# A two-layer encoder on one core: memory's keys and values ahead of the first projection, and row sums of the second layer taken from transposed quarters

## The chip, the core and the metric

The kernel runs on one core of a Trainium2 chip. The metric is the device time of one execution in microseconds (us). TensorE (PE in the profile; PEld are its weight loads) multiplies, VectorE (DVE) and ScalarE (ACT) work on whole tiles, GpSimd (POOL) does small arithmetic and issues the transfers that add while they move, and SyncE (SP) issues most loads and stores.

## What is computed

The input is 512 tokens by 1024 features, 256 memory tokens, and two layers of weights. Cut to what matters here:

```python
for i in range(2):
    h = rmsnorm(x, norm_g[i])
    mem_h = rmsnorm(mem, mem_norm_g[i])
    proj = einsum('bsd,de->bse', h, w_in)          # layer 0: 11264 columns, layer 1: 3584
    o_mix = mixer(...)                             # layer 0: dilated windows; layer 1: grouped queries with axial rotary
    kv = einsum('bnd,de->bne', mem_h, w_mem_kv[i]) # keys (normalized per head) and values of memory
    o_mem = attention(q_mem, k, v)
    y = concat([o_mix, o_mem]) * silu(gate)
    x = x + einsum('bse,ed->bsd', y, w_out[i])
```

Everything is float32. A product keeps that accuracy by splitting each operand into a high part (a rounded copy) and a low part (what the copy lost), and by summing three products: high by high, high by low, low by high.

## The kernel before

**Products.** `mm3` (lines 162 to 165) issues those three matmuls for one tile. A weight piece (128 x 1024, tile `wl`) is loaded, ACT makes its high part `wh` (`Weights.hi`, line 285), DVE its low part `wo` (`Weights.lo`, line 295). There are four buffers for `wh` and `wo`, so a cast waits until the matmuls of the piece four before it are done. Matmuls are issued in groups of twelve (128 x 512) or twenty-four (128 x 256); after each group `W.advance` issues the next pieces' low and high parts, sums and loads, and the driver's `tick` issues what is due of the evacuations, which are written as generators: `yield n` means "go on n groups later". All of it is one order written out by hand for each engine; each engine keeps to it.

**Seven products for eight.** The large projections (`s_chunk`) halve both operands in both directions and take seven products of quarters: of the activations the quarters 12, 11, 22 and the sums S1 to S4, of the weights the quarters 21, 11, 22 and the sums T1 to T4. Two pieces belong to each product when a chunk has 512 columns to a half (kinds W2 and W2s), one when it has 256. T2, T3 and T4 are made by transfers of POOL that add (lines 257, 264 and 269), T1 in layer 0 by DVE (line 251). In the very first chunk, number 0, DVE also makes T2 (line 259).

**Activations.** The blocks of x are normalized (`norm_1`: squares on ACT and three small operations on POOL; `norm_2`: two scalings of 128 x 512 on DVE, line 465). `turn4` transposes four 128 x 128 tiles on PE into one PSUM bank, ACT writes the high part (line 157), DVE the low part (line 160). `put_h` does that for one quarter of one pair of blocks. For S1 to S4 the sums are taken first, on the rows (`sum_h`, `sums_h`: DVE, lines 506 and 514 to 516), and each is then transposed as well: seven quarters by two blocks are 14 calls of `turn4`, 56 transposes, in either layer.

**The start.** x is loaded first, the first chunk is layer 0's projection of values (`ev_v0`, kind W2), and PE does `row_bank` (the gain row spread over 128 partitions by two matmuls of one row), transposes and then weights. Memory is loaded and normalized beside it (`mem_norm(0)`); its keys and values (`mem_kv`, two chunks of kind T2: two pieces for each of two units, two blocks) follow.

**Between the layers.** `out_rest` ends layer 0's output projection block by block, `ev_o` stores a block to `x1d`, normalizes it and puts its quarters, while PE works on memory's keys and values of layer 1 (two T2b chunks), and then on the seven products of memory's queries (24 matmuls of 128 x 256 to each). A small table for the rotary (`setup_b`, four DVE products) is made in the same place.

## Time and profile before

| | |
|---|---|
| median of 3 executions | 973.45 us (973.19 to 974.49) |
| the profiled execution, its own time | 971.6 us |
| span of it, first to last instruction | 969.8 us |
| PE busy | 949.5 us, 98% of the span |
| PEld, DVE, ACT, POOL busy | 835.8, 793.1, 675.4, 332.7 us |
| packets of SP's and ACT's queue, of POOL's | 43.5% and 32.5% of the 16 DMA engines' span |
| mean granted TensorE clock | 1.000 |

Matmuls overlap in the records: one of 128 x 512 is listed with 0.39 us while the next begins 0.23 us after it. So PE's pace is read from the starts of neighbouring rows, and idle time from what a view of the waits lists.

### The profile page before, as it was taken

The page shows a single profiled execution, that of the slowest core. Times are in us where ns is not written, and L with a number is a line of the kernel's source. Part 1 is how long each engine was busy: PE and PEld are TensorE (multiplying, and loading weights), DVE is VectorE, ACT ScalarE, POOL GpSimd, SP SyncE. Part 2 cuts the span into 40 slices and gives each one's busy share as a digit, 9 for nine tenths or more (in the row PEclk, how much of TensorE's full clock was granted, in tenths as well). Part 3 has the DMA queues.
Part 4 walks back from the last instruction along what each step waited for, and adds up shares of the span by engine and source line. Part 5 has one row for each costly group of instructions (what it writes and reads, how often), then busy time and mean ns, then how long its engine had stood idle before and what let it go on. Part 6 is the DMA issues. An engine that isn't in the chain of part 4 may idle for free. (4 is left out here: it accounts for less than half of the span.)

```text
span 969.8 us, 16665 instructions
## 1 busy us (share of the span) xinstructions
PE 949.5 (98%) x5728; PEld 835.8 (86%) x5728; DVE 793.1 (82%) x1413; ACT 675.4 (70%) x1687; POOL 332.7 (34%) x480
## 2 busy tenths in 40 slices
PE   8899999999999999999999999999999999999998
PEld 5689988888888888888899996787999999998776
DVE  6997776888888888888898999769888997779863
ACT  6555689686868686868685667545778887878760
POOL 1122423556454545454736011323233231011011
PEclk9999999999999999999999999999999999999999
DMA  8979846968787868685959889959986696786644
GB/s 331 326 267 336 220 102 170 293 131 259 150 256 154 256 153 261 154 260 131 279 134 233 259 203 272 299 191 351 240 178 148 178 241 166 218 213 163 183 140 130
DMA packets 88982, 209.27 MB, mean 216 GB/s; under 512 B 25281, under 2 KB 36033, under 8 KB 88898
## 3 DMA queue, kind: packets, MB, share of 16 engines
q1 hardware_dynamic: 70034, 146.28, 43.5%
q0 software_dynamic: 17568, 59.78, 32.5%
q10 hardware_dynamic: 1296, 2.16, 0.6%
q8 instruction: 45, 0.74, 0.3%
q14 instruction: 39, 0.32, 0.1%
HBM read 157.79 MB, written 12.65 MB: 176 GB/s over the span
## 5 line engine op out<-in xcount | busy, mean ns | idle before, releaser
L295 DVE TENSOR_TENSOR wo<-wl,wh 128x1024 fp32r<-128x1024 f32 x255 | 314.6, 1237 | 12.3 <-ACT wh L285 11.5
L285 ACT CAST wh<-wl 128x1024 fp32r<-128x1024 f32 x255 | 269.7, 1059 | 75.7 <-PE pj L165 39.8
L163 PE MATMUL pj<-wh,hS 128*128 128x512 f32 (+1 forms) x448 | 164.3, 367 | 0.0
L164 PE MATMUL pj<-wo,hS 128*128 128x512 f32 (+1 forms) x448 | 158.1, 353 | 2.6 <-DVE wo L295 2.6
L165 PE MATMUL pj<-wh,hS 128*128 128x512 f32 (+1 forms) x448 | 158.2, 353 | 0.0
L163 PE MATMUL pj<-wh,h 128*128 128x512 f32 (+1 forms) x336 | 123.4, 367 | 0.0
L164 PE MATMUL pj<-wo,h 128*128 128x512 f32 (+1 forms) x336 | 118.8, 354 | 2.3 <-DVE wo L295 2.3
L165 PE MATMUL pj<-wh,h 128*128 128x512 f32 (+1 forms) x336 | 118.9, 354 | 0.0
L420 POOL TENSOR_TENSOR rstd<-mse,half 128x4 f32<-128x4 f32 (+2 forms) x98 | 100.1, 1021 | 8.2
L164 PEld LDWEIGHTS pj<-wo,hS 128*128 128x128 f32 x448 | 85.0, 190 | 13.4 <-DVE wo L295 3.5
L165 PEld LDWEIGHTS pj<-wh,hS 128*128 128x128 f32 x448 | 84.7, 189 | 12.4 <-DVE hS L160 0.3
L163 PEld LDWEIGHTS pj<-wh,hS 128*128 128x128 f32 x448 | 84.8, 189 | 9.7
L419 POOL TENSOR_SCALAR mse<-hss 128x4 f32<-128x4 f32 (+1 forms) x86 | 44.3, 515 | 129.9 <-ACT junk L529 126.1
L360 ACT COPY sn<-pj 128x512 f32<-128x512 f32 x132 | 73.6, 591 | 14.3 <-PE pj L165 10.7
L529 ACT ACTIVATE junk<-sn 128x128 f32<-128x128 f32 x264 | 79.0, 308 | 0.2 <-DVE sn L371 0.2
L987 POOL TENSOR_TENSOR ta<-sn,tabs 128x128 f32<-128x128 f32 (+1 forms) x64 | 37.2, 584 | 119.7 <-DVE sn L534 91.6
L164 PEld LDWEIGHTS pj<-wo,h 128*128 128x128 f32 x336 | 64.0, 190 | 10.0 <-DVE wo L295 2.8
L165 PEld LDWEIGHTS pj<-wh,h 128*128 128x128 f32 x336 | 63.7, 190 | 9.3 <-DVE h L160 0.2
L163 PEld LDWEIGHTS pj<-wh,h 128*128 128x128 f32 x336 | 63.9, 190 | 7.3 <-ACT h L157 0.2
L377 DVE TENSOR_TENSOR sn<-pj,sn 128x512 f32<-128x512 f32 x99 | 67.5, 683 | 3.0 <-PE pj L165 2.6
L269 POOL DMA_DIRECT2D wl<-wl x33 | 29.3, 886 | 112.4 <-DVE wo L295 70.7
L163 PE MATMUL pj<-hS,wh 128*128 128x256 f32 x192 | 55.9, 291 | 0.0
(229 smaller groups left out, 2457.1 us busy)
## 6 DMA issues: line engine op xcount, KB each, us to landing
wl<-in_wall_dram SPq DMA_DIRECT2D x222, 512.0 KB, 6.9
wl<-wl POOLq DMA_DIRECT2D x64, 512.0 KB, 5.8
wl<-in_wall_dram POOLq DMA_DIRECT2D x42, 512.0 KB, 8.5
acc<-sn POOLq DMA_DIRECT2D x16, 256.0 KB, 5.0
od<-o SPq DMA_DIRECT2D x12, 256.0 KB, 5.2
og<-od SPq DMA_DIRECT2D x12, 256.0 KB, 6.8
odb<-o SPq DMA_DIRECT2D x12, 256.0 KB, 2.7
og<-odb SPq DMA_DIRECT2D x12, 256.0 KB, 3.9
```

The costliest lines, as they stand in the source:

```text
L163: T.matmul(o, lh, rh, start=start, stop=False, skip_group_check=True)
L164: T.matmul(o, lh, rl, start=False, stop=False, skip_group_check=True)
L165: T.matmul(o, ll, rh, start=False, stop=stop, skip_group_check=True)
L269: G.dma_start(self.tile[key], self.tile[c, "T2", x], accum_op=ALU.add)
L285: A.copy(wh, self.tile[self.items[i]])
L295: V.tensor_tensor(wo, self.tile[key], wh.bitcast(F32), ALU.subtract)
L360: A.copy(t, b)
L377: V.tensor_tensor(t, b, t, ALU.subtract if q == "12" else ALU.add)
L419: G.tensor_scalar(e, ss, EPS, None, ALU.add)
L420: G.tensor_tensor(r, e, half[:, 0:n], ALU.pow)
L529: A.activation(jk, p[:, j * 128:(j + 1) * 128], AF.Square, scale=QS, accum_out=ss[:, j:j + 1])
L987: G.tensor_tensor(ta[:, 0:n], xn[:, 0:n, 0:32], ropeA[:, 0, b, s0:s0 + n], ALU.mult)
```

## The change

It has these parts:

1. Memory's keys and values of layer 0 become PE's first work. Their rows and weights are loaded first (`SEQ` keeps the weights' places in memory, and changes the order of use), memory's gain row is spread first, x's gain row after it and copied to SBUF, memory is normalized at once, and x's blocks are normalized, transposed and summed in `prep` during memory's two chunks. The masks and rotary tables of layer 0 are loaded later, in `setup`.
2. `ev_v0`'s chunk follows. Its T2 sums are now made by POOL's transfer as in all other chunks; DVE's T1 stays.
3. In layer 1 only 12, 11, 22 and 21 are transposed: 8 calls of `turn4`. `first_t` keeps 12 and 11 as whole float32 tiles beside their high and low parts; `diffs_t` forms S1 = 21 - 22 and S3 = 11 - 21 from the transposed banks; `rest_t` makes S2 and S4 on whole tiles of 128 x 1024 and splits S2, S4, S3 and 22 in one piece of that size each.
4. In a chunk of memory or of the rest of an output projection, an evacuation is handed in before `W.advance` and its first step is issued before the next group's `W.advance` (`drv.release` for `drv.spawn`). The low part of memory's values is issued at the end of the same step as its high part, not a group later.
5. `EO` (gaps between the steps of `ev_o`), `SET_B` (when the rotary table of layer 1 starts), `PD`, `KEEP["T2"]` take other values.

```diff
-EO = 1, 2, 2, 2, 1
+EO = 2, 2, 1, 1, 1
+SEQ = [1, 2, 0] + list(range(3, len(PLAN)))
-KEEP = {"T2": 6, "T2b": 4, "O1": 4, "W1": 9, "W2": 10, "W2s": 9, "W1b": 7, "W2b": 9}
+KEEP = {"T2": 8, "T2b": 4, "O1": 4, "W1": 9, "W2": 10, "W2s": 9, "W1b": 7, "W2b": 9}
...
-                    if c:
-                        G.dma_start(self.tile[key], self.tile[c, "T1", x], accum_op=ALU.add)
-                    else:
-                        V.tensor_tensor(self.tile[key], self.tile[key], self.tile[c, "T1", x], ALU.add)
+                    G.dma_start(self.tile[key], self.tile[c, "T1", x], accum_op=ALU.add)
...
+                if pre:
+                    pre(u, b)
                 group(w, u, b, ps[b])
                 drv.free()
+                if u == units - 1:
+                    drv.release(evac(b, ps[b]), 2)
                 W.advance()
-                if u == units - 1:
-                    drv.spawn(evac(b, ps[b]), 2)
                 drv.tick()
...
+    def first_t(H, top, c):
+        ps = [(k, turn4(top[j], *slot(H, k, c))) for k, j in (("12", 1), ("11", 0))]
+        for k, p in ps:
+            A.copy(whole(k, c), p)
+
+    def diffs_t(H, low, c):
+        f22 = whole("22", c)
+        A.copy(f22, turn4(low[1], None, None))
+        p = turn4(low[0], None, None)
+        yield 1
+        s1, s3 = whole("S1", c), whole("S3", c)
+        V.tensor_tensor(s1, p, f22, ALU.subtract)
+        V.tensor_tensor(s3, full["11"][:, :, c * 128:(c + 1) * 128], p, ALU.subtract)
+        split(*slot(H, "S1", c), s1)
+
+    def rest_t(H, d):
+        def put(k, f):
+            H[k] = big(F32R, "h" + k).rearrange("p (a k t) -> p a k t", a=2, k=4)
+            split(H[k][:, 0], H[k][:, 1], f)
+        s2_, s4 = full["11"], full["12"]
+        V.tensor_tensor(s2_, full["S1"], s2_, ALU.subtract)
+        put("S2", s2_)
+        yield d
+        V.tensor_tensor(s4, s4, s2_, ALU.add)
+        put("S4", s4)
+        yield d
+        put("S3", full["S3"])
+        yield d
+        put("22", full["22"])
+        yield d
...
-    row0 = m4(name="row0")[0:1, :]
-    nc.sync.dma_start(row0, norm_g[0:1, :])
+    nc.sync.dma_start(row0, mem_norm_g[0:1, :])
+    nc.sync.dma_start(row1, norm_g[0:1, :])
+    for b in range(2):
+        nc.sync.dma_start(mt[b], mem[b * 128:(b + 1) * 128])
+        W.dma(1)
+    W.dma(2)
+    for c in range(4):
+        nc.sync.dma_start(xt[c], xv[c])
+        if c % 2:
+            W.dma(2)
...
-    first = row_bank("x0", WARM)
+    first = row_bank("m0", WARM)
+    gain = row_bank("x0", 1, pj)
...
-    drv.spawn(mem_norm(0), MEM_AT)
-    s_chunk(512, H, ev_v0, pre=second)
-    km, vm = mem_kv(0, Ms[0])
+    km, vm = mem_kv(0, M, ahead)
+    s_chunk(512, H, ev_v0)
...
             if b < 2:
-                put_h(H2, "12", b, x1[1])
-                put_h(H2, "11", b, x1[0])
+                first_t(H2, x1, b)
             else:
-                s1 = sum_h(x1)
-                yield EO[2]
-                sums_h(H2, x1b[b - 2], x1, b - 2, s1, sums_b)
+                yield from diffs_t(H2, x1, b - 2)
             if b == 3:
-                yield EO[3]
-                yield from rest_h(H2, sums_b, EO[4])
+                yield EO[2]
+                yield from rest_t(H2, EO[3])
```

The rows below are the order of instructions that each program holds, engine by engine; no time is in them. Between the first quarter of a chunk after the start and the end of layer 0, and from layer 1's second chunk on, the two orders are the same.

PE at the program's start, before (`row` is the gain row, `xT` a transposed block, `pj` a product, `wh` and `wo` the weight's parts):

```order
L562 MATMUL row_113<-row0_83,ones_73 128x512
L562 MATMUL row_112<-row0_83,ones_73 128x512
L886 MATMUL busy_116<-row0_83,ones_73 128x512
L471 MATMUL xT_135<-ident_68,x_78 128x128 x4
L886 MATMUL busy_140<-row0_83,ones_73 128x128
L163 MATMUL pj_164<-wh_130,h12_134 128x512
```

The same place now:

```order
L619 MATMUL row_115<-row0_85,ones_73 128x512
L619 MATMUL row_114<-row0_85,ones_73 128x512
L619 MATMUL row_119<-row1_87,ones_73 128x512
L619 MATMUL row_118<-row1_87,ones_73 128x512
L475 MATMUL xT_143<-ident_68,m_82 128x128 x4
L961 MATMUL busy_148<-row0_85,ones_73 128x128
L164 MATMUL pj_175<-wh_139,act_123 128x512
```

Four matmuls of a row stand ahead of the first transpose where three stood, and the first block is memory's.

DVE during memory's value chunk, now (`x_79` to `x_81` are x's second to fourth block, `xs1`, `xs2`, `xs4` sums of rows, `h12`, `h11`, `hS1` low parts of quarters, `xn` memory's keys being normalized):

```order
L513 TENSOR_TENSOR xs1_442<-x_81 128x512
L591 TENSOR_TENSOR xn_444<-pj_175,rstd_311 128x512
L297 TENSOR_TENSOR wo_435<-wl_188,wh_434 128x1024
L297 TENSOR_TENSOR wo_438<-wl_190,wh_437 128x1024
L161 TENSOR_TENSOR hS1_463<-xT_464,hS1_463 128x4x128
L521 TENSOR_TENSOR xs2_461<-xs1_404,x_78 128x512
L522 TENSOR_TENSOR x_80<-x_78,x_80 128x512
L523 TENSOR_TENSOR xs4_462<-x_78,xs2_461 128x512
L591 TENSOR_TENSOR xn_474<-pj_196,rstd_379 128x512
L161 TENSOR_TENSOR hS1_463<-xT_498,hS1_463 128x4x128
L521 TENSOR_TENSOR xs2_496<-xs1_442,x_79 128x512
```

`wo_435` and `wo_438` are the first two low parts of the value projection of x; before the change they came first of all weights, and memory's keys (`xn`) stood behind the whole of that projection.

DVE between the layers, before (`hS1`, `hS2`, `hS4` low parts from PSUM, `kmT` and `vm` low parts of memory's keys and values, `wo_8193` the low part of the fifth product's weight):

```order
L295 TENSOR_TENSOR wo_8094<-wl_7837,wh_8093 128x1024
L295 TENSOR_TENSOR wo_8097<-wl_7922,wh_8096 128x1024
L590 SCALAR_TENSOR_TENSOR kmT_7811<-qT_8099,gc_69,kmT_7810 128x4x128
L160 TENSOR_TENSOR hS2_8142<-xT_8143,hS2_8142 128x4x128
L160 TENSOR_TENSOR hS2_8142<-xT_8150,hS2_8142 128x4x128
L610 SCALAR_TENSOR_TENSOR vm_7813<-pj_7978,vm_7812 128x512
L590 SCALAR_TENSOR_TENSOR kmT_7811<-qT_8157,gc_69,kmT_7810 128x4x128
L160 TENSOR_TENSOR hS4_8196<-xT_8197,hS4_8196 128x4x128
L160 TENSOR_TENSOR hS4_8196<-xT_8204,hS4_8196 128x4x128
L610 SCALAR_TENSOR_TENSOR vm_7813<-pj_8014,vm_7812 128x512
L377 TENSOR_TENSOR sn_8190<-pj_8165,sn_8190 128x512
L295 TENSOR_TENSOR wo_8193<-wl_7924,wh_8192 128x1024
```

The same stretch now (`f11`, `f12` whole tiles; `wo_8111`, `wo_8114` and `wo_8203` are the low parts of the third, fourth and fifth product's weights):

```order
L571 TENSOR_TENSOR f11_7934<-fS1_8053,f11_7934 128x1024
L161 TENSOR_TENSOR hS2_8117<-f11_7934,hS2_8117 128x1024
L666 SCALAR_TENSOR_TENSOR vm_7816<-pj_7989,vm_7815 128x512
L297 TENSOR_TENSOR wo_8111<-wl_7841,wh_8110 128x1024
L297 TENSOR_TENSOR wo_8114<-wl_7912,wh_8113 128x1024
L647 SCALAR_TENSOR_TENSOR kmT_7814<-qT_8120,gc_69,kmT_7813 128x4x128
L574 TENSOR_TENSOR f12_7932<-f12_7932,f11_7934 128x1024
L161 TENSOR_TENSOR hS4_8165<-f12_7932,hS4_8165 128x1024
L666 SCALAR_TENSOR_TENSOR vm_7816<-pj_8034,vm_7815 128x512
L647 SCALAR_TENSOR_TENSOR kmT_7814<-qT_8168,gc_69,kmT_7813 128x4x128
L161 TENSOR_TENSOR hS3_8206<-fS3_8054,hS3_8206 128x1024
L381 TENSOR_TENSOR sn_8200<-pj_8175,sn_8200 128x512
```

Each sum now stands directly ahead of its own low part, with ACT's cast between the two, and both S2's sum and its low part stand ahead of the third product's weight. The row after the last is `wo_8203`.

More of the change, by code (lines that the diff above doesn't have):

```diff
@@ L209, in __init__ @@
                             g += 1
-            assert d == wall.shape[0], (d, wall.shape)
+            assert sum(pieces(k) for k in PLAN) == wall.shape[0]
             self.g = -1
@@ L329, in trunk_kernel, with chunk @@
     W = Weights()
-    def chunk(units, nb, group, evac):
+    def chunk(units, nb, group, evac, pre=None):
         ps = [None] * nb
@@ L555, in row_load, with row_bank @@
         rows[name] = halves(t)
-    def row_bank(name, times=1):
-        r = [at("row") for _ in range(2)]
+    def row_bank(name, times=1, bank=at):
+        r = [bank("row") for _ in range(2)]
         for j in (1, 0):
@@ L880, in setup @@
             yield 1
-    first = row_bank("x0", WARM)
+    first = row_bank("m0", WARM)
+    gain = row_bank("x0", 1, pj)
+    rows["x"] = halves(m4(name="row"))
     def busy(n):
-        T.matmul(at("busy")[:, 0:n], ones, rows["x0"][0][0:1, 0:n], start=True, stop=True)
-    busy(512)
-    nst[0] = norm_1(xb[0], True)
+        T.matmul(at("busy")[:, 0:n], ones, rows["m0"][0][0:1, 0:n], start=True, stop=True)
+    mb, M = [halves(t) for t in mt], Act(NM)
+    nst = [norm_1(mb[0], True)]
     W.hi(True)
-    norm_2(xb[0], nst[0], first, (1,))
+    norm_2(mb[0], nst[0], first, (0,))
     def mid():
@@ L895, in mid, with ahead @@
         W.lo()
-        nst[1] = norm_1(xb[1], BOTH)
-    put_h(H, "12", 0, xb[0][1], mid, True)
-    if W_EARLY:
-        W.hi(True)
-    norm_2(xb[1], nst[1], first, (1,))
-    norm_2(xb[0], nst[0], first, (0,))
-    norm_2(xb[1], nst[1], first, (0,))
-    def second():
-        put_h(H, "12", 1, xb[1][1])
-        if not W_EARLY:
-            W.hi(True)
-        put_h(H, "11", 0, xb[0][0])
-        nst[2] = norm_1(xb[2], BOTH)
-        W.lo()
-        put_h(H, "11", 1, xb[1][0])
-        W.hi(True)
-        nst[3] = norm_1(xb[3], BOTH)
+        nst.append(norm_1(mb[1]))
+    turn4(mb[0][0], M.block(0, 0, slice(0, 128)), M.block(1, 0, slice(0, 128)), mid)
+    W.hi(True)
+    norm_2(mb[1], nst[1], first, (0,))
+    W.lo()
+    def ahead(u, b):
+        if (u, b) == (0, 1):
+            for j in range(2):
+                A.copy(rows["x"][j], gain[j])
+            norm_3(mb[1], M, 128, 0)
+            for c in range(2):
+                norm_2(mb[c], nst[c], first, (1,))
+        if (u, b) == (1, 0):
+            for c in range(2):
+                norm_3(mb[c], M, 128 * c, 1)
     drv.spawn(prep(), PD)
@@ L1185, in trunk_kernel @@
     row_load("x1", norm_g[1:2, :])
-    x1b, sums_b = {}, []
     def ev_o(n, b, x1):
```

78 lines of the change are left out of this document (50 added, 28 removed).

## The prediction

> **What bounds the kernel now.** I read the page first, then busy time by stretch, then PE's waits by stretch, then the order of time in the two places that the change touches.
>
> ```profile
> span 969.8 us, 16665 instructions
> PE 949.5 (98%) x5728; PEld 835.8 (86%) x5728; DVE 793.1 (82%) x1413; ACT 675.4 (70%) x1687; POOL 332.7 (34%) x480
> ```
>
> PE is the bound over the whole: only PE time that disappears, or PE idle time that disappears, can shorten the span. The stretches (columns: stretch, its length, busy time of PE, PEld, DVE, ACT, POOL, granted clock, DMA share, GB/s) show where that is open:
>
> ```profile
> 0.00:16.00 16.00, 12.77 (x33) 7.51 (x34) 7.46 (x13) 8.54 (x18) 2.22 (x11) 1.00 0.89 334
> 16.00:46.00 30.00, 25.42 (x129) 20.25 (x127) 28.53 (x36) 16.95 (x27) 6.01 (x10) 1.00 0.99 317
> 577.00:647.00 70.00, 67.20 (x317) 53.86 (x316) 59.89 (x93) 37.97 (x62) 14.41 (x20) 1.00 0.84 249
> 657.60:687.10 29.50, 28.32 (x181) 24.79 (x180) 29.41 (x41) 17.78 (x39) 8.75 (x10) 1.00 1.05 331
> ```
>
> From 16 to 46 DVE is busy 28.5 of 30 us, from 657.6 to 687.1 it is busy 29.4 of 29.5: **in both places DVE paces PE**. PE's waits say the same, first from 0 to 46, then from 647 to 699:
>
> ```profile
> PE pj L164 <- DVE wo L295: 4.6, 4, 2.0
> ...
> PE pj L164 <- DVE wo L295: 0.8, 2, 0.5
> PE qT L541 <- DVE xn L534: 0.3, 1, 0.3
> ```
>
> **The paces** that the sums use come from rows with more than one piece, or from the start of a row to the start of the next:
>
> ```profile
> 10.39 2.06 DVE L465 SCALAR_TENSOR_TENSOR x<-x,rstd,row 128x512 f32<-128x512 f32 x3
> 36.10 2.00 ACT L285 CAST wh<-wl 128x1024 fp32r<-128x1024 f32 x2 [1.97 <-DVE wl L259]
> 38.20 1.07 ACT L157 CAST hS<-xT 128x512 fp32r<-128x512 f32 x2
> 38.85 1.28 DVE L160 TENSOR_TENSOR hS<-xT,hS 128x512 fp32r<-128x512 f32 x2
> 40.05 2.35 DVE L295 TENSOR_TENSOR wo<-wl,wh 128x1024 fp32r<-128x1024 f32 x2
> 41.59 1.03 PE L471 MATMUL xT<-ident,x 128*128 128x128 f32 x8
> 42.38 0.48 PE L163 MATMUL pj<-wh,hS 128*128 128x512 f32 x1
> 17.20 0.63 ACT L458 ACTIVATE sq<-x 128x512 f32<-128x512 f32 x1
> 17.64 0.39 PE L164 MATMUL pj<-wo,h 128*128 128x512 f32 x1
> 17.86 0.39 PE L165 MATMUL pj<-wh,h 128*128 128x512 f32 x1
> ```
>
> DVE: 0.70 us a scaling, 0.60 a half tile (38.85 to 40.05 for two), 1.14 a whole tile. ACT: 1.0 a whole tile, 0.5 a half tile. PE: eight transposes 0.79 us (41.59 to 42.38), a matmul 0.227, so a group of twelve 2.72.
>
> **Part 1, the start.** PE now spreads two gain rows before its first transpose:
>
> ```profile
> 2.24 3.75 PE L562 MATMUL row<-row,ones 1*128 1x512 f32 x4 [2.24 <-DMA row<-in_norm_g_dram]
> 5.78 1.91 PE L886 MATMUL busy<-row,ones 1*128 1x512 f32 x2
> 7.87 1.11 PE L471 MATMUL xT<-ident,x 128*128 128x128 f32 x4 [0.17 <-DVE x L465]
> 9.02 0.58 ACT L157 CAST h<-xT 128x512 fp32r<-128x512 f32 x1
> 9.65 0.80 PE L163 MATMUL pj<-wh,h 128*128 128x512 f32 x1
> 11.53 0.63 PE L164 MATMUL pj<-wo,h 128*128 128x512 f32 x1
> 11.96 0.63 PE L165 MATMUL pj<-wh,h 128*128 128x512 f32 x1
> ```
>
> Each of the row matmuls is two passes of 0.85 us (four from 2.24 to 5.78, less the first's longer start). There were six passes, there are eight: the transposes can start at 2.24 + 0.1 + 8 x 0.85 = 9.2 instead of 7.87, the first weight matmul, 1.78 later as before, at 11.0 instead of 9.65. That is 1.3 us lost. It starts at half pace: 11.53 to 11.96 is 0.43 a matmul, against 0.227 at 17.64, though the granted clock reads 1.00. Half pace lasted from 9.65 to between 12 and 15 us; I take 3.4 to 4 us of it again. Then twelve matmuls end at 15.3. Transposes (0.4) and ACT's cast behind them (0.9) put the second group at 16.7; with 0.25 of waiting for its low part it ends at 19.6. Eight transposes and a cast (1.3) put the third at 20.9, and it and the fourth end at 26.6 (0.25 + 2 x 2.72); ACT then makes a weight cast (1.0) and two squares (0.63 each) before it casts x's first quarter, and DVE's low part of it can begin at 29.4. From there DVE is full: up to x's second S2 row sum the order holds six whole tiles, four scalings and fourteen half tiles, 6 x 1.14 + 4 x 0.70 + 14 x 0.60 = 18.0 us, to **47.4**. PE has done memory's four value groups by 39.5, waits 1.0 us for a row sum and 0.6 for the first low part of the next weight, issues one group (to 45.0), and waits until 47.4 for that S2 row sum, whose transposes stand ahead of the next group. After that it has 13 groups and 24 + 8 transposes: 48.2 + 13 x 2.72 + 2.4 = **86.0**. Before, the same work was done here:
>
> ```profile
> 85.97 0.60 PE L541 MATMUL qT<-ident,xn 128*128 128x128 f32 x4
> ```
>
> with two sets of four transposes of keys (0.35 each) still to come, so 86.7. The start gives **-0.7 us**, or +0.1 if half pace lasts 0.8 us longer; I take -0.3. Bounds: -2.5 (ACT's casts come a group sooner and DVE's backlog starts at 27.4) to +2.0 (every group until the fourth waits as long again for its cast as the second). The waits on `wo` at 22 to 39 us go, and a row sum that is late at 47 takes their place.
>
> The Trainium skill, "TensorE: Matmul & The Clock Gate", section "What's actually happening", says that activity releases a halved clock after one window of about 3.4 us, and that the windows run freely. The trace speaks against counting one-row matmuls as activity, since those from 2.24 on left the first dense group at 0.43; counted from the first dense group, the rule fits. By it full pace comes between 14.4 and 17.8, and the start gives between -0.7 and +0.1.
>
> **Part 2, T2 of the first chunk by transfer.** It takes two whole tiles (2.3 us) off DVE; that is in the count above. The price, as issue, size in KB and us to landing:
>
> ```profile
> wl<-wl POOLq DMA_DIRECT2D x64, 512.0 KB, 5.8
> ```
>
> These two start when T1 is there (34.0 and 38.5 us) and serve a cast due at 57: about 13 us of cover, so nothing. If the cover went, S2's first group would wait for what the transfer is late.
>
> **Part 3, between the layers.** PE loses six calls of four transposes, 6 x 0.395 = 2.4 us. DVE's rows:
>
> ```profile
> 647.91 1.06 ACT L285 CAST wh<-wl 128x1024 fp32r<-128x1024 f32 x1 [0.31 <-PE pj L165]
> 657.65 1.42 DVE L465 SCALAR_TENSOR_TENSOR acc<-acc,rstd,row 128x512 f32<-128x512 f32 x2 [1.45 <-DMA x1d<-acc]
> 667.33 0.93 POOL L257 DMA_DIRECT2D wl<-wl  x1 [2.42 <-DMA wl<-in_wall_dram]
> 668.98 1.34 POOL L420 TENSOR_TENSOR rstd<-mse,half 128x4 f32<-128x4 f32 x1
> 676.85 1.05 ACT L285 CAST wh<-wl 128x1024 fp32r<-128x1024 f32 x1 [4.02 <-DMA wl<-wl]
> 680.47 0.74 DVE L590 SCALAR_TENSOR_TENSOR kmT<-qT,gc,kmT 128x512 fp32r<-128x512 f32 x1
> 681.13 1.27 DVE L160 TENSOR_TENSOR hS<-xT,hS 128x512 fp32r<-128x512 f32 x2
> 685.98 1.20 DVE L295 TENSOR_TENSOR wo<-wl,wh 128x1024 fp32r<-128x1024 f32 x1
> 690.04 0.36 PE L163 MATMUL pj<-wh,hS 128*128 128x256 f32 x1
> 690.24 0.28 PE L164 MATMUL pj<-wo,hS 128*128 128x256 f32 x1
> ```
>
> Before, DVE works without a hole from 657.65 to 687.1, the end of the fifth product's `wo`, and PE uses that at 690.24: 3.1 us of slack. Now, from the cast that ends at 648.97: two low parts to 650.7; block one's and two's scalings, the gain, two tables, two low parts and block one's quarters (1.4 + 0.25 + 0.6 + 1.4 + 0.6 + 2.3 + 1.2) to **658.4**. From there to the same `wo` the order holds 26.8 us: twelve whole tiles, seven of them weights (13.7), four scalings (2.8), four differences from PSUM (2.4), nine further half tiles (5.4) and four low parts of memory's keys and values (2.5; 680.47 to 681.13 for one). Added are the **holes**, where DVE stands behind ACT because the next row is a low part whose high part isn't cast: the second block's quarters, behind four copies, four squares and two weight casts on ACT (2 us); S1 twice (0.1 each); S2, where ACT's queue holds the T2 weight ahead of S2's cast; S4 (1.0); S3 (0.6). T2's cast waited for a transfer until 676.8 before. It now stands on POOL behind a second `rstd` that it preceded before, which ends near 667.5, so 9.4 us later it lands at 676.4 to 677: S2's cast ends at 678.4 to 679, and DVE, ready at 676.4, has a hole of 2 to 2.6. Together 5.8 to 6.4: the `wo` ends at 658.4 + 26.8 + 6.1 = **691.3**, and PE's second matmul of the fifth product starts there, not at 690.24: **+1.1 us**, and +1.4 where the later end of T2 holds. I take +1.3. PE arrives early (its transposes are gone) and waits. Bounds: if the holes vanish, DVE is there at 685.2 and PE gains its 2.4 us and the 1.1 us of waits listed above, -3.5; with T2 a further 2 us late, +3.3.
>
> **Parts 4 and 5.** The earlier first steps of evacuations are additions and squares on DVE and ACT in stretches where PE waits for neither (ACT is busy 38 of the 70 us from 577 to 647); moved tables are counted above. Nothing else changes place, so 86 to 640 and 700 to the end keep their time.
>
> **Sum.** -0.3 + 1.3 = +1.0 us on the profiled execution's 971.6, so 972.6. The median of the three is 1.9 us above that execution; the same step puts the median at **974.5**.
>
> **Rivals.**
> - *Faster: ACT's queue is not in the way.* For it: ACT is busy only 17.8 of the 29.5 us, and DVE has 2.7 us less work in the stretch. If the transfer of T2 lands by 674 and the second block's quarters follow at once, the holes shrink by 4 us or more, the fifth `wo` comes at 687, and PE keeps its saving: -2.4 to -3.5 there, -0.3 at the start, so 969.7 to 970.8; with the start's lower bound as well 967.5. Against it: the handoffs of S2, S4 and S3 have no other row between sum, cast and low part.
> - *Slower: DVE's backlog at the start is larger.* One mechanism: the first quarter of x on DVE waits for ACT, which waits for PE's fourth group, which began 1.3 us later and at half pace. It decides once that low part begins after 30.5 us rather than 29.4, each later microsecond being a microsecond of PE. With half pace for all twelve (to 16.1) and one more late cast it begins near 31.2: +1.5 at the start, +1.4 between the layers, so 976.4.
> - *It does not do what it says at the start:* memory first only moves the DVE backlog behind memory. The sum above says that nearly so; an exact swap is 0 there, 974.8, within the forecast.
>
> **How the numbers follow.** A measurement of this kernel tells about 0.2%, 1.95 us, from no change. Forecast (971.5 to 975.4, the swap in it): 0.45. Faster rival: 0.27. Slower rival: 0.28. The range that leaves out about 2 in 10 takes in both rivals' times: 969.0 to 977.5. The forecast's own range is 972.5 to 975.4.
>
> **What would show it.** Right: the first weight matmul near 11 us; a PE wait for DVE's row sums near 45 to 48; the end of the first seven products near 86; 32 transposes instead of 56 between the layers, with holes in DVE ended by ACT at S2, S4, S3, and PE waiting over 3 us on `wo` of the fourth or fifth product near 687 to 691. Wrong: no hole of DVE there and the fifth product's start before 688.5 (then the faster rival), or PE idle in the first 90 us above 20 us (then the slower).

## The result and the profile after

The changed kernel took **980.57 us** in the median of six executions (979.47 to 984.71), the kernel before 973.79 in six taken beside it (971.29 to 974.72): a ratio of 1.0081, 95% interval 1.0066 to 1.0096. It is slower by 0.8%, and outside the range that was forecast (969.0 to 977.5). The profiled execution took 979.47 us, 7.9 more than that of before. Its page begins:

```profile
span 977.6 us, 16643 instructions
PE 952.0 (97%) x5706; PEld 837.0 (86%) x5706; DVE 789.6 (81%) x1405; ACT 679.7 (70%) x1691; POOL 342.8 (35%) x482
```

PE has 22 matmul records fewer and is busy 2.5 us longer, a first sign that something made its matmuls slower. Busy time by stretch, as before (length, PE, PEld, DVE, ACT, POOL, granted clock, DMA share, GB/s):

```profile
0.00:16.00 16.00, 13.71 (x30) 7.47 (x30) 5.27 (x9) 7.09 (x13) 2.18 (x10) 1.00 0.87 335
16.00:46.00 30.00, 26.37 (x128) 20.25 (x126) 26.44 (x34) 23.31 (x54) 14.53 (x19) 1.00 0.93 333
577.00:650.00 73.00, 69.90 (x333) 56.33 (x333) 60.20 (x93) 41.15 (x67) 14.50 (x21) 1.00 0.84 245
660.70:693.60 32.90, 26.32 (x165) 23.50 (x164) 27.87 (x36) 22.95 (x45) 8.26 (x10) 0.95 0.98 289
```

The last row holds the loss between the layers: PE idles 6.6 of 32.9 us, and the granted clock is 0.95. To place the loss I use four marks that both traces have: the start of the first run of 96 matmuls of 128 x 256, the first group of memory's T2b chunk in layer 1, the first transposes of queries behind the next seven products, and the end of the span.

| stretch, us | before | after | difference |
|---|---|---|---|
| start to the first run of 96 | 92.58 | 95.38 | +2.80 |
| to the T2b chunk | 555.08 | 555.35 | +0.27 |
| to the transposes of queries (between the layers) | 53.97 | 58.36 | +4.39 |
| to the end | 268.17 | 268.51 | +0.34 |

Two of the four carry 7.2 of 7.8 us. PE's waits there, as instruction, what it waited for by the profile, us in total, times, longest; up to 90 us and from 640 to 705:

```profile
PE pj L164 <- DVE xn L591: 2.7, 1, 2.7
...
PE pj L164 <- ACT h L158: 5.9, 1, 5.9
PE pj L165 <- DVE wo L297: 0.7, 1, 0.7
```

**The start.** Neither of the two long waits is for the row sum that the prediction named. These are the rows that lead up to the first one, of DVE and then of PE:

```profile
11.17 0.79 PE L164 MATMUL pj<-wh,act 128*128 128x512 f32 x1
...
30.06 1.29 DVE L161 TENSOR_TENSOR h<-xT,h 128x512 fp32r<-128x512 f32 x2 [1.51 <-ACT h L158]
...
43.98 0.68 DVE L161 TENSOR_TENSOR hS<-xT,hS 128x512 fp32r<-128x512 f32 x1
44.58 0.68 DVE L521 TENSOR_TENSOR xs<-xs,x 128x512 f32<-128x512 f32 x1
45.18 0.68 DVE L522 TENSOR_TENSOR x<-x 128x512 f32<-128x512 f32 x1
45.78 0.69 DVE L523 TENSOR_TENSOR xs<-x,xs 128x512 f32<-128x512 f32 x1
46.38 0.68 DVE L591 TENSOR_TENSOR xn<-pj,rstd 128x512 f32<-128x512 f32 x1
...
47.58 0.68 DVE L521 TENSOR_TENSOR xs<-xs,x 128x512 f32<-128x512 f32 x1
...
47.12 0.51 PE L164 MATMUL pj<-wh,h 128*128 128x512 f32 x1 [2.71 <-DVE xn L591]
48.60 1.89 PE L475 MATMUL xT<-ident,xs 128*128 128x128 f32 x8
```

PE issued the first half of the first group of values' projection and stopped. The other half goes into the second of the two banks, and that bank still held the keys of memory's second block: DVE reads them in `xn` (46.38), which stands behind a low part and three row sums. So a matmul waited for an **evacuation of its own output bank**, a kind of wait that the prediction had not looked for. The row sum that it had named (x's second S2 sum, the last DVE row shown) ended at 48.26, and its transposes began at 48.60, when PE came to them.

**Between the layers.** The same kind, and longer:

```profile
680.72 1.23 DVE L161 TENSOR_TENSOR hS<-f,hS 128x1024 fp32r<-128x1024 f32 x1 [1.12 <-ACT hS L158]
...
682.46 2.35 DVE L297 TENSOR_TENSOR wo<-wl,wh 128x1024 fp32r<-128x1024 f32 x2
...
685.39 1.22 DVE L574 TENSOR_TENSOR f<-f,f 128x1024 f32<-128x1024 f32 x1
687.72 1.22 DVE L161 TENSOR_TENSOR hS<-f,hS 128x1024 fp32r<-128x1024 f32 x1 [1.11 <-ACT hS L158]
...
690.67 1.23 DVE L161 TENSOR_TENSOR hS<-fS,hS 128x1024 fp32r<-128x1024 f32 x1 [0.47 <-ACT hS L158]
691.81 0.68 DVE L381 TENSOR_TENSOR sn<-pj,sn 128x512 f32<-128x512 f32 x1
692.41 1.22 DVE L297 TENSOR_TENSOR wo<-wl,wh 128x1024 fp32r<-128x1024 f32 x1
...
691.48 1.05 ACT L158 CAST h<-f 128x1024 fp32r<-128x1024 f32 x1
...
686.47 0.28 PE L166 MATMUL pj<-wh,hS 128*128 128x256 f32 x1
692.64 0.55 PE L164 MATMUL pj<-wh,hS 128*128 128x256 f32 x1 [5.89 <-ACT h L158]
693.00 0.41 PE L165 MATMUL pj<-wo,hS 128*128 128x256 f32 x1
693.21 0.41 PE L166 MATMUL pj<-wh,hS 128*128 128x256 f32 x1
...
697.33 0.28 PE L165 MATMUL pj<-wo,hS 128*128 128x256 f32 x1
```

The third product (S1) issues its last matmul at 686.47, and the fourth (S2) begins at 692.64. The low part of its weight was there at 684.8 and S2's own at 681.95. The profile names a cast of ACT that ended at 692.53, but the fourth product reads nothing of it: that is the last quarter's. What ended within 0.1 us of that cast is `sn` on DVE (691.81 to 692.49). It matters because of one entry in the table of products, in both kernels:

```python
PRODUCTS = (("12", 0, True), ("11", 1, True), ("S1", 0, True), ("S2", 1, False), ...
```

`False` means that S2's product goes on adding in the bank in which 11's product stands. `sn` reads that bank for 11 alone, so it has to be done first. Before, `sn` stood behind two low parts of S4 too, but was done at 686.05, in time for the fourth product at 686.30:

```profile
685.38 0.67 DVE L377 TENSOR_TENSOR sn<-pj,sn 128x512 f32<-128x512 f32 x1
...
686.30 0.36 PE L163 MATMUL pj<-wh,hS 128*128 128x256 f32 x1
```

**The clock.** Behind either wait PE runs at half pace: matmuls of 128 x 256 start 0.21 us apart at 693, and 0.12 at 697. Here the granted clock shows it (same columns as above):

```profile
44.00:48.00 4.00, 1.29 (x6) 0.75 (x5) 4.00 (x8) 0.00 (x0) 0.08 (x1) 1.00 1.04 310
48.00:52.00 4.00, 4.00 (x19) 3.64 (x17) 4.00 (x6) 1.79 (x4) 2.69 (x3) 0.58 1.09 254
52.00:56.00 4.00, 4.00 (x23) 3.41 (x22) 3.90 (x7) 2.07 (x5) 0.00 (x0) 1.00 1.06 211
...
686.00:692.00 6.00, 0.75 (x7) 0.55 (x5) 4.42 (x6) 5.36 (x7) 0.00 (x0) 0.86 1.05 297
692.00:697.00 5.00, 4.36 (x20) 4.39 (x21) 5.00 (x5) 3.13 (x11) 1.69 (x2) 0.50 1.03 404
697.00:701.00 4.00, 4.00 (x35) 4.00 (x34) 0.32 (x2) 1.89 (x3) 2.75 (x3) 0.98 0.85 242
```

The fourth product, 24 matmuls, took from 692.64 to 697.2, 4.6 us instead of 2.95: 1.6 us on top of the wait.

### The profile page after: what moved, and what is told of

The parts are those of the page before. It is cut to its first block, busy times and chain, and to the rows that moved or that the text cites. A ratio compares the mean times of both kernels' runs of the same rounds, so it can differ in the third digit from the quotient of the medians.

```text
span 977.6 us, 16643 instructions
## 1 busy us (share of the span) xinstructions
PE 952.0 (97%) x5706; PEld 837.0 (86%) x5706; DVE 789.6 (81%) x1405; ACT 679.7 (70%) x1691; POOL 342.8 (35%) x482
## 5 line engine op out<-in xcount | busy, mean ns | idle before, releaser
L424 POOL TENSOR_TENSOR rstd<-mse,half 128x4 f32<-128x4 f32 (+2 forms) x98 | 104.2, 1064 | 8.2
L164 PEld LDWEIGHTS pj<-wh,hS 128*128 128x128 f32 x448 | 85.8, 192 | 16.0 <-ACT h L158 6.1
L166 PEld LDWEIGHTS pj<-wh,hS 128*128 128x128 f32 x448 | 85.7, 191 | 12.3
L165 PEld LDWEIGHTS pj<-wo,hS 128*128 128x128 f32 x448 | 86.0, 192 | 10.9 <-DVE wo L297 0.9
```

Source lines behind the costliest of these rows:

```text
L164: T.matmul(o, lh, rh, start=start, stop=False, skip_group_check=True)
L165: T.matmul(o, lh, rl, start=False, stop=False, skip_group_check=True)
L166: T.matmul(o, ll, rh, start=False, stop=stop, skip_group_check=True)
L424: G.tensor_tensor(r, e, half[:, 0:n], ALU.pow)
```

## The experiments

**Theory A**: both losses come from the order of DVE's rows, in which an evacuation that PE's next group needs stands behind rows that nobody needs yet; the halved clock follows from the idling. Its rivals: one loss that shifts the other (B), DVE and ACT simply full (C), another cause of the clock (D), and those named at each run. Every ratio is to the kernel before, run beside it. The sets of runs were taken apart from each other, so gains over after are given by the difference of the two ratios (one thousandth is 0.97 us).

| kernel | median, us | before, us | ratio, 95% interval | start, us | between the layers, us |
|---|---|---|---|---|---|
| after | 980.57 | 973.79 | 1.0081 (1.0066 to 1.0096) | 95.38 | 58.36 |
| old_start | 979.25 | 972.55 | 1.0067 (1.0050 to 1.0084) | 92.51 | 60.65 |
| old_rows | 974.66 | 972.55 | 1.0021 (1.0007 to 1.0035) | 95.50 | 54.47 |
| old_evac | 981.53 | 971.96 | 1.0094 (1.0076 to 1.0112) | 95.07 | 60.11 |
| r3111 | 974.76 | 972.55 | 1.0027 (1.0012 to 1.0042) | 97.23 | 54.28 |
| t2_dve | 983.08 | 971.96 | 1.0104 (1.0085 to 1.0123) | 96.79 | 57.83 |
| hold2 | 977.44 | 972.31 | 1.0056 (1.0035 to 1.0076) | 94.54 | 59.00 |
| gain_later | 984.07 | 971.96 | 1.0116 (1.0098 to 1.0134) | 99.13 | 58.38 |
| gain_dma | 980.44 | 972.04 | 1.0075 (1.0060 to 1.0091) | 93.39 | 58.73 |
| fill | 982.48 | 972.55 | 1.0092 (1.0070 to 1.0114) | 94.86 | 60.31 |
| fill40 | 977.31 | 972.04 | 1.0049 (1.0034 to 1.0065) | 94.76 | 56.38 |
| both | 972.21 | 972.31 | 0.9999 (0.9985 to 1.0013) | 94.07 | 54.12 |
| rows_only_late | 974.66 | 972.31 | 1.0021 (1.0003 to 1.0038) | 92.70 | 52.77 |
| both_e2 | 973.61 | 972.31 | 1.0005 (0.9989 to 1.0020) | 93.06 | 53.46 |
| best | 972.89 | 971.96 | 1.0005 (0.9990 to 1.0020) | 92.38 | 52.18 |
| all_three | 969.23 | 972.04 | 0.9969 (0.9958 to 0.9980) | 92.66 | 52.20 |

The last two columns are the first and third row of the table of stretches, from the one profiled execution of each.

### One half of the change at a time

**old_start**: the start of before with the new part between the layers and the new evacuations. **old_rows**: after, with `ev_o`, `EO` and `SET_B` as before. **old_evac**: after, with the steps of the evacuations as before:

```diff
-                if u == units - 1:
-                    drv.release(evac(b, ps[b]), 2)
                 W.advance()
+                if u == units - 1:
+                    drv.spawn(evac(b, ps[b]), 2)
...
```

> The part between the layers alone (quarters transposed first, sums behind them, and the evacuations handed out a step earlier), with the start of before. In the profiles of before and after, PE gets 2.9 us later up to the end of the first two chunks, 4.4 us between the layers, and 0.5 us in the rest. Theory A (two separate losses, each from PE waiting for DVE to empty the bank that the next group writes): 973.8 + 4.4 = 978 us, between 977.4 and 978.8, with PE idle about 6 us ahead of the fourth product and the granted clock at 0.50 behind that. Rival B (one loss: the start shifts transfers, and the boundary is late only because of that): at most 975.

> The start alone (memory first, T2 by transfer, earlier evacuations), with row sums before the transposes between the layers as before. Theory A: 973.8 + 2.9 = 976.7 us, between 976 and 977.5, and the end of the first two chunks near 89.6 us. Rival B (the loss at the boundary comes from what the start changes): 979 to 981.

> After, with the first steps of the evacuations of memory's chunks and of the output's back where they were before (a step later, and the low part of values in a step of its own). The prediction put this part at nothing: 980.6 within 0.7 us. Theory A: the same, since on DVE the order around the two late evacuations hardly changes. Rival H (the earlier steps crowd DVE and ACT ahead of the sums): 979 or less.

The part between the layers alone costs 6.7 us, the start alone 2.1: together 8.8, against 7.9 by the ratio of the whole (1.0081 of 973). So the losses are separate, and rival B falls. The sizes were off by one to two us, and both times lie outside their expected ranges. In old_start's trace the transfer that makes T2 takes 9.5 us instead of 7.3, ACT holds S2's cast behind that weight's cast, DVE holds behind S2's low part the second reading of memory's values, and S1's first matmul, which takes the values' bank, waits 1.5 us for that: a third evacuation of the same kind, here late by a transfer. old_evac cannot be told from after in time, but its trace is not the same: PE waits 8.2 us ahead of the third product instead of 5.9 ahead of the fourth.

### The order of DVE's rows between the layers

**r3111**: after, with one line of `rest_t` changed. S4, S3 and 22 come two groups later, so `sn` stands ahead of S4's sum.

```diff
         put("S2", s2_)
-        yield d
+        yield d + 2
```

> After, with S4, S3 and the last quarter two steps later, so that on DVE the evacuation that the fourth product waits for stands ahead of S4's sum and low part. Theory A (the order of DVE's rows makes the wait): the evacuation ends near 687.3 instead of 692.4, PE idles under 2 us ahead of the fourth product and the clock stays at 1.00; the fifth product starts near 692 instead of 697.2: 980.6 - 5 = 975.5 us, between 974.5 and 976.5. Rival C (DVE and ACT have too much work there, in whatever order): the wait moves to the fifth product, whose sum and low part are now behind the evacuation, and the time stays within 1 us of 980.6.

```profile
689.11 0.38 PE L164 MATMUL pj<-wh,hS 128*128 128x256 f32 x1 [0.63 <-DVE sn L381]
692.94 0.38 PE L164 MATMUL pj<-wh,hS 128*128 128x256 f32 x1 [0.71 <-ACT sn L364]
```

With nothing taken away, the wait ahead of the fourth product fell from 5.9 to 0.6 us, now named `sn` by the profile as well, that ahead of the fifth is 0.7, and the granted clock doesn't fall behind either. By the ratios the time fell by 5.2 us. Rival C falls for this place. So does the profile's own attribution to a cast of ACT, since here the fourth product starts at 689.11, while on ACT even S4's cast, two casts ahead of the last quarter's, begins at 691.36 only.

### DVE's queue at the start

**t2_dve** puts a suspected cost back: T2 of the first chunk is added on DVE, as it was before. **hold2** only reorders: the row sums of x come two groups later.

```diff
-                    G.dma_start(self.tile[key], self.tile[c, "T1", x], accum_op=ALU.add)
+                    if c:
+                        G.dma_start(self.tile[key], self.tile[c, "T1", x], accum_op=ALU.add)
+                    else:
+                        V.tensor_tensor(self.tile[key], self.tile[key], self.tile[c, "T1", x], ALU.add)
```

```diff
             yield 1
+        yield 2
         for c in range(2):
             sums_h(H, xb[c], xb[2 + c], c, s1[c], sums)
```

> After, with T2 of the first chunk added on DVE again: two more whole tiles (2.3 us) on DVE, both ahead of the sums' end at 49.5 us, one of them ahead of the key evacuation that PE waits for at 47 us; two transfers fewer. Theory A (DVE's queue up to the second set of sums paces PE there): 980.6 + 2.3 = 982.9 us, between 981.8 and 984, and the wait at 44 us grows to about 3.9 us. Rival G (PE's own backlog paces the first chunks): within 0.7 us of 980.6.

> After, with one more step of two groups before the row sums of the first chunk, so that on DVE the second block's key evacuation and the next two low parts of weights stand ahead of the sums; nothing is added or taken away. Theory A: the 2.7 us wait at 44 us is for that evacuation, which stood behind three sums; now PE runs from 42.4 to about 53 without it, the clock stays at 1.00, and the first two chunks end near 85.3 instead of 89.6 us: 980.6 - 4.3 = 976.3 us, between 975 and 977.5. Rival C (DVE has too much to do there in any order): PE waits as long for the first weight behind the sums, and the time stays above 979.5.

In t2_dve's timeline one of the two whole tiles stands ahead of `xn`:

```profile
44.13 1.22 DVE L264 TENSOR_TENSOR wl<-wl 128x1024 f32<-128x1024 f32 x1
...
47.67 0.68 DVE L594 TENSOR_TENSOR xn<-pj,rstd 128x512 f32<-128x512 f32 x1
...
48.40 0.53 PE L164 MATMUL pj<-wh,h 128*128 128x512 f32 x1 [3.84 <-DVE xn L594]
```

PE's wait grew from 2.71 to 3.84 us by that one tile (1.14), as theory A had it. The time grew by 2.2 us by the ratios, which is not clear of noise, and its trace doesn't place all that it shows here: the start grew by 1.4 us only, and 3.5 more lie behind the queries' transposes (272.1 against 268.5 us). hold2 took the wait for `xn` of the second block away and 2.4 us off the time by the ratios (3.1 by the medians), at the edge of noise and less than the 4.3 expected: its waits show another one, of 2.0 us until 43.22, ahead of the transposes of the first block's `xn`, which after starts at 41.94. The clock was halved behind it from 44 to 48 us (0.57), although this wait is so short.

```profile
PE qT L598 <- DVE xn L591: 2.0, 1, 2.0
```

The start column mixes three things: when DVE begins with x's low parts, DVE's order, and the clock. Counted from DVE's first low part of x to the mark, they come apart:

| kernels | stretches of 3.41 us at half clock | first low part of x to the mark, us |
|---|---|---|
| fill (22 fillers in the wait), fill40, old_evac | 0 | 64.3, 64.3, 64.6 |
| after, old_rows, gain_later, gain_dma | 1 | 65.3 to 65.4 |
| r3111 | 2 | 66.4 |
| t2_dve (one tile more ahead of `xn`) | 1 | 66.6 |
| hold2, both, both_e2, all_three (row sums later) | 1 | 62.8 to 63.2 |

So a halved stretch costs about 1.05 us here, the tile 1.2, and the later row sums save 2.1 us or more with nothing taken away: rival C falls for the start too, in the traces.

### The first weight matmul's 1.5 us

**gain_later** issues the two row matmuls of x's gain behind the first group instead of ahead of memory's transposes. **gain_dma** drops them and their two copies on ACT; a transfer spreads the row.

```diff
+        if c == 0:
+            row_load("x", norm_g[0:1, :])
...
-    gain = row_bank("x0", 1, pj)
```

> After, with the two row matmuls that spread x's gain behind the first group of weights instead of ahead of memory's first transposes, so that PE's first weight matmul starts near 9.8 us instead of 11.2, as before. The prediction's step says that this lateness passes on whole (1.3 us): 979.3 us. Theory A says that DVE's queue sets the end of the stretch, and that it starts on x's low parts (30.1 us) behind PE's third group and ACT: the row matmuls only move to where PE waits 0.8 us for a cast, so 0 to 0.6 us are gained, 980.0 to 980.6.

> After, with x's gain row spread over the partitions by a transfer of 512 KB, queued behind the first quarter of x, instead of by two row matmuls and two copies on ACT. PE's first weight matmul then starts near 9.8 us instead of 11.2. The prediction's step (this lateness passes on whole, through PE's groups and ACT to DVE's first low part of x): 980.6 - 1.3 = 979.3 us, and DVE's first low part of x at 28.7 instead of 30.1 us. Rival J (x's and the weights' transfers or the reciprocal root on POOL hold the stretch up anyway, or the added transfer does): within 0.5 us of 980.6 or above.

gain_later missed, since it changed something else: the first group had just reached full pace (0.23 at 13.97), and with four passes of one-row matmuls, four transposes and a wait of 1.06 us behind that the clock was halved for the whole second group. DVE's first low part of x came at 33.85 instead of 30.06, the mark 3.75 us later, and the kernel is 3.4 us slower than after by the ratios: this lateness did pass on whole.

```profile
17.00:20.00 3.00, 1.94 (x5) 1.45 (x5) 1.86 (x3) 3.00 (x6) 0.00 (x0) 0.53 1.03 410
20.00:24.00 4.00, 4.00 (x12) 3.09 (x11) 2.42 (x3) 1.23 (x4) 1.96 (x3) 0.50 1.02 418
```

In gain_dma's trace PE and DVE are both 1.8 to 2.0 us earlier than after, from the first weight matmul (11.17 in after) to the first low part of x (30.06) and on to the end of the stretch (93.39 against 95.38):

```profile
9.35 0.79 PE L164 MATMUL pj<-wh,act 128*128 128x512 f32 x1
...
28.04 1.29 DVE L161 TENSOR_TENSOR h<-xT,h 128x512 fp32r<-128x512 f32 x2 [1.50 <-ACT h L158]
```

So in the trace the 1.8 us pass on whole, as the prediction's step said. The median does not confirm it: 980.44 is that of after within 0.2 us (0.6 by the ratios), and the profiled execution, 977.48, is the shortest of six that reach up to 981.5. For the row matmuls' own 1.5 us the time stays open.

### What idling costs in clock

**fill** and **fill40** are after with matmuls into a spare bank where PE waits: 22 and 48 of 128 x 256, or 40 between the layers alone.

```diff
+    def keep_busy(act, n):
+
+        p = at("busy")[:, 0:256]
+        for _ in range(n):
+            T.matmul(p, act["12"][:, 0, 0, 0:128], act["12"][:, 0, 0, :], start=True, stop=True)
...
+                if fill == a:
+                    keep_busy(act, 40)
...
-    s_chunk(256, H2, ev_qmb)
+    s_chunk(256, H2, ev_qmb, fill="S2")
```

> After, with 22 (first chunk) and 48 (between the layers) matmuls of 128x256 into a spare bank, whose result nothing reads, issued where PE idles 2.7 and 5.9 us; DVE's and ACT's rows keep their order. Theory A says that idling halves the clock behind it: 20 matmuls at 0.212 instead of 0.12 between the layers (1.9 us), and about 1.3 us in the first chunk. The granted clock then stays at 1.00 at 48 to 52 and 690 to 697 us, and the time is 980.6 - 3.2 = 977.4 us (976.4 to 978.6). Rival D (the halved clock has another cause): the clock dips as before, and the time is 980.6 or more.

> After, with 40 matmuls of 128x256 into a spare bank ahead of the fourth product alone (4.8 of the 5.9 us in which PE idles there; nothing reads their result). Theory A: the clock stays at 1.00 behind the wait, the fourth product takes 2.95 instead of 4.6 us, and the time is 980.6 - 1.7 = 978.9 us. Rival D (the clock dips all the same, or the fillers delay the product by as much): 980.6 or more.

fill missed: T2's transfer between the layers landed 10.2 us after its issue, so S1 waited 2.6 us and ran at a halved clock (0.57 from 684 to 688), and the 48 fillers then ended 1.5 us behind the evacuation. fill40 answered the question:

```profile
684.97 4.96 PE L356 MATMUL busy<-h 128*128 128x256 f32 x40
691.03 0.35 PE L164 MATMUL pj<-wh,hS 128*128 128x256 f32 x1 [1.11 <-ACT h L158]
691.23 0.28 PE L165 MATMUL pj<-wo,hS 128*128 128x256 f32 x1
```

```profile
686.00:692.00 6.00, 4.89 (x41) 4.72 (x41) 5.42 (x7) 6.00 (x9) 0.00 (x0) 1.00 1.03 333
692.00:697.00 5.00, 5.00 (x44) 5.00 (x44) 3.43 (x4) 3.07 (x11) 3.29 (x4) 1.00 0.95 361
```

Useless work in the wait kept the clock at 1.00, the fourth product took 2.95 us, and the stretch 2.0 us less than after. The time fell by 3.1 us by the ratios; what is more than the stretch isn't explained. In all seven traces in which a wait of 4.5 us or more stood there unfilled, the clock was halved behind it. Rival D falls for this place.

### Putting the orders together

**both** is hold2 with r3111's line. **rows_only_late** is old_start with it. **both_e2** is both with S2's sum and cast one group earlier. **best** is rows_only_late with S2's put moved so, but behind the second `xn` on DVE. **all_three** is hold2 with gain_dma's transfer and best's order between the layers:

```diff
-                yield EO[2]
                 yield from rest_t(H2, EO[3])
...
-        put("S2", s2_)
-        yield d
+        drv.late(lambda: put("S2", s2_))
+        yield d + 3
```

> The two reorderings (sums of the first chunk later, S4 later) together. Theory A: the losses are separate and both come from DVE's order: 980.6 - 4.3 - 5.5 = 970.8 us, 1.8 us under before (972.6 in the last comparison), between 969.5 and 972. Rival C or a loss common to both: 974 or more.

> Start of before, quarters transposed first between the layers, S4 later. In the profile of r3111 the stretch between the layers took 54.3 us, against 54.0 before and 58.4 after, though PE has 2.4 us less to do there: theory A gives 972.6 + 0.3 = 972.9 us, between 972 and 974 (no gain: the T2 transfer, the cast of S2 behind it and S4's chain of sum, cast and low part eat the 2.4 us). Rival E (r3111 was disturbed by its later start): PE's saving is kept, 970.5 or less.

> As both, with S2's sum and cast one step earlier, so that on ACT the cast of S2 stands ahead of the T1 and T2 weights' casts, and on DVE the evacuation of memory's values, which S1's first matmul waits for, no longer stands behind the landing of T2. Theory A: the holes of 1.1 to 2.6 us on DVE at S2 and the waits of 0.9 to 2.5 us ahead of S1 go, 1.3 to 2 us of them on PE's path: 970.8 - 1.5 = 969.3 us, between 968 and 970.5. Rival F (T2's landing binds through S2's own weight): equal to both within 0.4 us.

> Start of before; quarters transposed first between the layers; S4 after the evacuation that the fourth product waits for, and S2's cast and low part one step earlier, behind the second key evacuation on DVE and ahead of the weights' casts on ACT. Theory A: of the 54.0 us between the layers in before, PE has 2.4 us less to do; the waits of 0.9 and 0.8 us ahead of the third and fourth product in rows_only_late go, about 1 us stays at the fifth: 52.3 us, so 972.3 - 1.6 = 970.7 us, between 969.7 and 971.7. Rival C (DVE and ACT are full there whatever the order): the waits move to the fifth product, and the time is that of before within 0.5 us.

> After with the gain by transfer, the sums of the first chunk two steps later, and S2 earlier and S4 later between the layers as in best. Theory A: the first stretch is then that of before within 0.7 us (95.4 - 1.3 - 1.2 = 92.9 against 92.6 us), and 1.8 us are gained between the layers as in best's profile (52.2 against 54.0): 972.0 + 0.3 - 1.8 = 970.5 us, between 969.5 and 971.8. Rival K (what best showed: the time in the profile is gained, but waits and clock elsewhere give it back): 972 to 974.

The losses add up in reverse too: both is 8.0 us under after by the ratios and equal to before. From after over both and both_e2 to all_three the stretch between the layers fell step by step, 58.4, 54.1, 53.5 and 52.2 us, but the time did not follow each step. both_e2 (973.61), rows_only_late (974.66) and best (972.89) all lie above the ranges expected of them and show no gain on before (both missed its range by 0.2 us): rows_only_late is slower by 0.21%, though its traced stretch is 1.2 us shorter. In all_three 0.7, 0.6 and 0.3 us of waits are left ahead of the fifth product, the fourth, and within the fifth:

```profile
PE pj L164 <- ACT sn L364: 0.7, 1, 0.7
PE pj L164 <- DVE sn L381: 0.6, 1, 0.6
PE pj L166 <- DVE hS L161: 0.3, 1, 0.3
```

That is 1.8 us under before, most of the 2.4 us of transposes that the change saves. **all_three is faster than both kernels** in the median: 969.23 us, 0.31% under before (interval 0.20 to 0.42%), and 1.1% under after by the two ratios. Its 2.8 us are more than the 1.8 that the stretches show, and best, with the same stretches, shows no gain: its twelve executions spread from 969.4 to 976.8 us, those of all_three from 968.5 to 972.3. Before's spread like best's (970.4 to 975.9). So where all_three's gain comes from isn't shown. Its trace is of a long execution (971.68) and has the same span as that of before, 969.8 us: the 1.8 us gained between the layers are lost again behind the queries' transposes (269.85 against 268.17 us). PE waits there, at 913 us, 1.6 us for a `sn` that stands on DVE behind the landing of a load. In the seventeen traces that wait is anything from nothing to 2.5 us, so it is one thing in which executions differ; that it makes the long ones long isn't shown.

## Why the prediction was wrong

The forecast gave +1.0 us on the profiled execution; it was +7.9. Step by step:

1. **First weight matmul at 11.0 instead of 9.65**: right (11.17), and the trace of gain_dma bears out that this passes on.
2. **DVE full up to x's second S2 row sum, at 47.4**: right, and 0.9 us short. The sum ended at 48.26. DVE's first low part of x began at 30.06 instead of 29.4, and from there the counted six whole tiles, four scalings and fourteen half tiles took 18.2 us, where 18.0 were reckoned.
3. **"PE ... issues one group (to 45.0), and waits until 47.4 for that S2 row sum"**: this step failed at the start. PE issued half a group and waited to 47.1 for `xn`. Every read of DVE that the sum looked at was an operand of PE; that a bank has to be emptied before PE writes it again was left out. That the end of the wait was nearly right is luck: the `xn` that held PE and the sum that was forecast to hold it end 1.2 us apart.
4. **The end at 86.0**: 89.6. The transposes of S2 began at 48.60 instead of 47.4 (1.2 us). The clock was halved behind the wait, and up to 55.09 PE took 1.8 us longer than at the prediction's paces. The sum had no term for that; it had one for the cold start alone. Four transposes of keys (0.36) were left out, and a group took 2.75 us instead of 2.72 (about 0.3 in all).
5. **T2 by transfer costs nothing and takes 2.3 us off DVE**: not contradicted. In t2_dve, where it is undone, DVE's first low part of x and the mark are 1.2 us further apart at the same clock, the worth of one of the two tiles; the other 1.1 us don't show there.
6. **Holes of DVE behind ACT between the layers, 5.8 to 6.4 us**: they were 2.14, 1.12, 1.11 and 0.47, 4.8 in all, at the places named. With marks shifted by the 3.1 us of the start, the fifth product's `wo` was forecast to end at 694.4 and ended at 693.6: right, a little too late.
7. **"PE's second matmul of the fifth product starts there"**: this is the step that failed between the layers. DVE's queue was followed to the right row and 0.8 us too far, but PE needs the row just ahead of it, `sn`, a whole product earlier. Shifted by the start, the fourth product began at 689.6 instead of 686.3 (+3.3) and its clock was halved (+1.6). With the eight transposes gone that stood ahead of the fifth, that one began 4.1 us late, and 4.4 stood at the end of the stretch, where +1.3 was forecast.
8. **The earlier evacuations cost nothing**: in time not told apart from nothing (old_evac).

Of the rivals, the slower one had the right sign at the start and too small a price. Its condition, a first low part of x "after 30.5 us", wasn't met (30.06), and its sign, PE idle for over 20 us up to 90 us, didn't come either (7.0 us); the price came from elsewhere. The exact swap did not happen. The faster one had the holes of DVE shrink by 4 us or more; at 4.8 us they were nearer to the forecast, and holes were not what decided.

The rule of the Trainium skill, "TensorE: Matmul & The Clock Gate", section "HAM oscillation — how this bites in real kernels", that idle gaps of PE over some 3.4 us halve the clock again, was not weighed in the prediction, though its own signs named a PE wait of over 3 us between the layers. The 5.9 us wait agrees with it. The 2.0 and 2.7 us waits, behind which the clock also read 0.57 and 0.58 over 4 us, are shorter than its bound, and there the measurement decides.

## What to carry to other kernels

When a change puts work into an engine's queue, list not only the operands that wait behind it but every evacuation: a matmul that adds on in a bank, or takes a bank over, waits for its readers, and the profile may name another row that ended at the same time. Then look at which of the rows ahead of the evacuation are needed later than it is; here lengthening one `yield` was worth 5.2 us. And price a wait of PE of about 2 us or more with its length and, as a risk, up to half of the 3.41 us behind it.

## What the runs showed of the hardware that was not expected

- A wait well under 3.4 us can halve the clock. Behind the 2.7 us wait that begins at 42 to 48 us it was halved in five of seven traces (after, old_rows, r3111, gain_dma, gain_later, but not old_evac and fill40); behind the 2.0 us wait that ends at 41 to 43 us in all four (hold2, both, both_e2, all_three); behind waits of 1.8 to 2.1 us that begin at 23 us in none of four (before, old_start, rows_only_late, best). That it hangs on more than the length is shown, on what it hangs isn't.
- In the clock records of the seventeen traces every halved stretch that doesn't run into the end of the program lasts 3.41 us, or two or three times that (6.83, 10.24). After and r3111 run the same program up to the stretch between the layers and wait the same 2.71 us at the start, but got one such stretch and two; their first low parts of x are 0.8 us apart and their marks 1.85.
- Work of one row did not keep the clock up: in gain_later 1.9 us of row matmuls and 1.7 of transposes and waiting between two dense groups were followed by 0.50 through the next 5 us. This is one trace.
- The same transfer of 512 KB between the layers (T2's) took 7.3, 9.4, 9.5 and 10.2 us in after, r3111, old_start and fill, and it goes with what SP issues beside it. In the nine traces in which it took 7.3 to 8.1 us, SP's next weight load is issued 0.8 us or more behind it. In seven others a third load stands ahead of it or up to 0.1 us behind, and it took 9.2 to 10.9 us. Before fits neither (9.4 us, the next load 0.9 us behind). No run moved that load alone, so this is not shown to be the cause.
